# A hybrid RWKV-7 and sliding-window decoder block in exact float32: the early up blocks' second product added at once, and the row-factor passes set in a fixed order

## The chip, the cores and the metric

One core of a Trainium2 chip runs the whole program. The metric is the time of one execution on the device in microseconds (us), as the median of several runs. Instructions are issued in order on each engine: TensorE (PE: matmuls, and PEld: weight loads), VectorE (DVE), ScalarE (ACT), GpSimd (POOL) and SyncE (SP). In this kernel POOL and SP do little more than start transfers.

## The reference

The block takes `x` of 512 rows by 2048 columns. It is normalised and multiplied by `w_in`; RWKV-7 time mixing and sliding-window attention work on the result; gates merge the two, `w_out` brings them back, and the sum with `x` is `x1`. The stage of this change begins there: `x1` is normalised by its root mean square and `norm2_g`, multiplied by `w_up` (2048 by 2 x 5632), passed through a causal convolution of width 3 along the rows, gated, and multiplied by `w_down`.

```python
x = x + (g_rw * p_rw + g_att * p_att) @ w_out[l]
x = x + conv_ffn(rms_norm(x, norm2_g[l]), w_up[l], conv_w[l], conv_b[l], w_down[l])
# conv_ffn(h, ...):
u = h @ w_up
up = jnp.pad(u, ((0, 0), (CONV_W - 1, 0), (0, 0)))
c = up[:, 0:S] * conv_w[0] + up[:, 1:S + 1] * conv_w[1] + up[:, 2:S + 2] * conv_w[2] + conv_b
val, gate = jnp.split(c, 2, axis=-1)
return (jax.nn.silu(gate) * val) @ w_down
```

## The kernel before

**Products.** The three large products after attention (`w_out`, `w_up`, `w_down`) are made by a Strassen-Winograd scheme: both factors are cut in quarters, and seven products of quarters (with sums of quarters as factors) take the place of eight. Float32 accuracy comes from splitting each factor into a high and a low part, so that one product is three matmuls per tile: high by high, high by low, low by high.

**The up stage.** `w_up` is worked in 44 blocks, one per 128 value columns and the 128 gate columns that go with them. A block `f` has the seven products P1, P2, P7, P6, P5, Q4, P3, and one of them is 24 matmuls of 128x128 by 128x256. `parts` (L1087, L1088) splits the weights of a product: ACT writes the rounded high part `whi`, then DVE subtracts for the low part `wlo`. For P6 and P3 DVE first adds two quarters (`sums`, L1081). `hlp` has three buffers for the split weights, so the split of a product waits until the product three before it is through. The weights come by SP in 512 KB quarters (L1072) into a ring of six `raw` buffers and two `a11` buffers; for `s1` and `s3` POOL then starts a second transfer that adds another quarter on arrival (L1074). A load is issued when a buffer becomes free.

**Row factors.** The other factor is the normalised `x1`, in quarters `q11`, `q12`, `q21`, `q22` (in the rows of instructions: `x_13037`, `x_13038`, `x_13039`, `x_13040`). They are transposed on PE, and `transposed` copies the result from PSUM times `norm2_g`, half of the copies on ACT and half on DVE. For `q12` and `q22` the transposing matmul is against a diagonal that holds the rows' scale (`dg`). Sums of quarters are the factors `t3`, `t1`, `t2`, `t4`, each an op on DVE over 128x2048. Every factor is then split by `split_q`: high part on ACT (L1052, 1.9 us), low part on DVE (L1053, 2.3 us). `b11` belongs to P1, `b21` to P2, `t3` to P7, `t2` to P6, `t1` to P5, `t4` to Q4, `b22` to P3.

**Order of products.** The first four blocks are the early ones: P1 for all four, then P2 for all four, then P7, since `b11` and `b21` are there first. Then come the remaining products of blocks 0 and 1 in turns, P6(0), P5(0), P6(1), P3(0), P5(1), Q4(0), P3(1), Q4(1), and the same for blocks 2 and 3. From block 4 on all seven follow each other. In an early block P1 goes to one half of a PSUM bank (`X`) and is copied to `t1`-named tile `t_15888` and so on by ACT (L1114); P2 goes to the other half of the same bank (`Z`), and P6 and P5 later accumulate on `X`. The sum of both, the first part of `u`, is written by DVE from the copy and from `Z` (`B[f].out("P2")`, L1125): for blocks 0 and 1 just ahead of P6(0), for 2 and 3 after P6(2) and Q4(2). While the main loop runs, `prep` for product i+2 (sum and split) is written ahead of the matmuls of product i, and the copies out of PSUM (`out`, L1121 to L1125) behind them.

**What sets the order.** The kernel is built on a scheduler that may reorder instructions inside an engine. `pin` keeps an instruction in the order of the source; the matmuls, weight splits and copies out are pinned, the row-factor ops (`transposed`, `split_q`, the sums of quarters) are not. `reuse_waits` on the pools makes a new tile wait until the last user of the memory is through.

## Time and profile before

| | us |
|---|---|
| median of 3 runs | 2936.24 (2934.93 to 2939.33) |
| the profiled execution's own time | 2935.18 |
| its span, first to last instruction | 2933.4 |
| PE busy | 2879.3 (98%) |
| DVE busy | 1959.2 (67%) |
| ACT busy | 1319.0 (45%) |

The profiled execution is 1.06 us under the median. Times in the rows are counted from the start of the span. PE is busy for 98% of it, so it is the few gaps of PE that can be won or widened, and they differ from stage to stage. The early up blocks lie between 1595 and 1700 us.

### The profile page before, as it was taken

To read this page: it belongs to the slowest core of one execution; us is meant where nothing else is said; L and a number is where in the kernel's file an instruction comes from. 1 tells how busy PE (TensorE), PEld (TensorE's weight loads), DVE (VectorE), ACT (ScalarE), POOL (GpSimd) and SP (SyncE) were. 2 spreads that over 40 slices of the span, in tenths; PEclk is the share of its full clock that TensorE was granted. 3 is DMA by queue.
4 is the path that set the end of the run, shared out by engine and by line. 5 is a ranking of instruction groups with operands and counts; after the bars stand their busy time and mean duration, and the time that the engine had idled before them with its cause. 6 is when DMAs were issued, how large, how long until landed. Compare 5 with 4: busy or idle time off the path is not lost.

```text
span 2933.4 us, 48233 instructions
## 1 busy us (share of the span) xinstructions
PE 2879.3 (98%) x18810; PEld 2453.2 (84%) x18810; DVE 1959.2 (67%) x3250; ACT 1319.0 (45%) x2134; POOL 219.4 (7%) x288
## 2 busy tenths in 40 slices
PE   7999999999999999999999899999999999999999
PEld 6777777777777777788888899999999999888887
DVE  5565666667667666345567877777877877665555
ACT  4344434434434434232356555555555554544444
POOL 0001000000000000101000011101101010000000
PEclk9999999999999999999999999999999999999999
DMA  6865656656656656878877788888889888877785
GB/s 184 212 152 149 175 141 159 162 134 160 163 138 160 158 139 168 274 217 247 286 249 236 195 234 238 237 230 226 226 236 242 233 227 228 313 239 243 255 258 188
DMA packets 225141, 609.39 MB, mean 208 GB/s; under 512 B 24768, under 2 KB 44944, under 8 KB 223888
## 3 DMA queue, kind: packets, MB, share of 16 engines
q1 hardware_dynamic: 157504, 434.86, 46.8%
q0 software_dynamic: 36064, 132.14, 23.5%
q10 hardware_dynamic: 31344, 39.31, 3.9%
q8 instruction: 147, 2.41, 0.3%
q14 instruction: 82, 0.67, 0.1%
HBM read 556.56 MB, written 174.43 MB: 249 GB/s over the span
## 4 chain that ended last, share of the span: by engine, by line
PE 91%; DVE 3%; DMA 3%; ACT 2%; issue 1%; ACTq 0%; SPq 0%; DVEq 0%; POOLq 0%
PE X L1105 16%; PE X L972 11%; PE acc L261 11%; PE acc L260 10%; PE acc L259 10%; PE Y L972 8%; PE Y L1105 8%; PE Z L1105 4%; PE bulk L686 1%; DMA raw<-in_w_up_dram 1%; PE mi L504 1%; PE bulk L748 1%; PE psG L755 1%; PE psS L766 1%; PE bulk L725 1%
## 5 line engine op out<-in xcount | busy, mean ns | idle before, releaser
L259 PE MATMUL acc<-xhi,whi 128*128 128x512 f32 x1120 | 456.1, 407 | 5.2 <-ACT whi L242 5.2
L261 PE MATMUL acc<-xhi,wlo 128*128 128x512 f32 x1120 | 459.4, 410 | 1.7 <-DVE wlo L243 1.7
L260 PE MATMUL acc<-xlo,whi 128*128 128x512 f32 x1120 | 452.7, 404 | 0.0
L242 ACT ACTIVATE whi<-raw 128x512 fp32r<-128x512 f32 x352 | 220.1, 629 | 478.0 <-PE acc L260 368.5
L965 DVE TENSOR_TENSOR wlo<-raw,whi 128x1024 fp32r<-128x1024 f32 x210 | 257.1, 1225 | 203.6 <-ACT whi L964 201.9
L243 DVE TENSOR_TENSOR wlo<-raw,whi 128x512 fp32r<-128x512 f32 x352 | 239.8, 688 | 198.9 <-ACT whi L242 191.2
L964 ACT ACTIVATE whi<-raw 128x1024 fp32r<-128x1024 f32 x210 | 222.6, 1060 | 289.1 <-PE X L972 150.6
L1105 PE MATMUL X<-b,whi 128*128 128x256 f32 x1472 | 269.2, 283 | 2.3 <-DVE u L1125 0.9
L1105 PE MATMUL X<-t,whi 128*128 128x256 f32 x1408 | 259.8, 285 | 10.1 <-DVE u L1125 9.6
L1088 DVE TENSOR_TENSOR wlo<-raw,whi 128x1024 fp32r<-128x1024 f32 x176 | 215.0, 1223 | 77.0 <-ACT whi L1087 76.9
L1105 PE MATMUL Y<-t,whi 128*128 128x256 f32 x1408 | 257.2, 283 | 0.0
L259 PEld LDWEIGHTS acc<-xhi,whi 128*128 128x128 f32 x1120 | 211.3, 189 | 44.8 <-ACT whi L242 6.4
L261 PEld LDWEIGHTS acc<-xhi,wlo 128*128 128x128 f32 x1120 | 211.0, 188 | 44.9 <-DVE wlo L243 4.4
L260 PEld LDWEIGHTS acc<-xlo,whi 128*128 128x128 f32 x1120 | 211.0, 188 | 40.4 <-issue 1.6
L1087 ACT ACTIVATE whi<-a 128x1024 fp32r<-128x1024 f32 x132 | 139.4, 1056 | 216.6 <-DVE a L1081 214.7
L1105 PEld LDWEIGHTS X<-b,whi 128*128 128x128 f32 x1472 | 229.5, 192 | 3.1 <-issue 2.4
L1105 PEld LDWEIGHTS X<-t,whi 128*128 128x128 f32 x1408 | 221.7, 194 | 10.7 <-DVE u L1125 7.1
L1105 PEld LDWEIGHTS Y<-t,whi 128*128 128x128 f32 x1408 | 219.6, 192 | 0.0
L1105 PE MATMUL X<-b,wlo 128*128 128x256 f32 x736 | 208.5, 283 | 2.3 <-DVE wlo L1088 2.3
L1088 DVE TENSOR_TENSOR wlo<-a,whi 128x1024 fp32r<-128x1024 f32 x132 | 161.7, 1225 | 67.4 <-ACT whi L1087 66.7
L1105 PE MATMUL X<-t,wlo 128*128 128x256 f32 x704 | 200.4, 285 | 0.2 <-DVE wlo L1088 0.2
L1105 PE MATMUL Y<-t,wlo 128*128 128x256 f32 x704 | 199.2, 283 | 0.0
(347 smaller groups left out, 6117.7 us busy)
## 6 DMA issues: line engine op xcount, KB each, us to landing
raw<-in_w_up_dram SPq DMA_DIRECT2D x180, 512.0 KB
raw<-in_w_z_dram SPq DMA_DIRECT2D x288, 256.0 KB
s_dn<-in_w_dn_dram POOLq DMA_DIRECT2D x88, 512.0 KB, 6.7
raw<-in_w_up_dram POOLq DMA_DIRECT2D x88, 512.0 KB, 8.6
raw<-s_dn SPq DMA_DIRECT2D x88, 512.0 KB
raw<-in_w_dn_dram SPq DMA_DIRECT2D x66, 512.0 KB
a<-in_w_up_dram SPq DMA_DIRECT2D x48, 512.0 KB
s_dn<-in_w_dn_dram SPq DMA_DIRECT2D x44, 512.0 KB
```

Of the source, the lines that this page charges most:

```text
L242: pin(act.activation(hi, raw, AF.Copy))
L243: pin(dve.tensor_tensor(lo, raw, hi.bitcast(F32), op=ALU.subtract))
L259: pe.matmul(acc, whi[:, j], xhi[:, k], start=first, stop=False)
L260: pe.matmul(acc, whi[:, j], xlo[:, k], start=False, stop=False)
L261: pe.matmul(acc, wlo[:, j], xhi[:, k], start=False, stop=last)
L504: pe.matmul(ps[:, h], pT[:, kb, h], vt[:, n - 1 + kb, g * HD : (g + 1) * HD], start=kb == kbs[0], stop=kb == kbs[-1])
L964: act.activation(whi, wr, AF.Copy)
L965: dve.tensor_tensor(wlo, wr, whi.bitcast(F32), op=ALU.subtract)
L972: pe.matmul(dst, l[:, q, ts], r[:, es], start=fst and j == 0, stop=lst and j == 2, skip_group_check=True)
L1087: pin(act.activation(hi, t, AF.Copy))
L1088: pin(dve.tensor_tensor(lo, t, hi.bitcast(F32), op=ALU.subtract))
L1105: pin(pe.matmul(ps, l[:, k], r[:, k], start=start and k + i == 0, stop=last and i == 2, skip_group_check=True))
```

## The change

1. In `transposed`, DVE takes one copy in four instead of one in two when the diagonal is used (`q12`, `q22`), ACT the others; these copies are pinned.
2. All row-factor ops are pinned. `split_q` falls into `high` (ACT) and `low` (DVE), and they are written in a fixed order around the products: at most one factor's pass per product.
3. In an early block, P2 is added to the ACT copy of P1 as soon as it is there (`self.t1 += Z`, DVE). `begin` later copies that sum into `u` on ACT, without reading PSUM. Four adds and four copies take the place of four adds.
4. The last factor's split (`t4`) is moved behind P6(0) and P5(0); the factor `q21` stays ahead of P6(0) in the source.

```diff
             dst = q[:, 2 * k // KH, k % (KH // 2) * TH : (k % (KH // 2) + 1) * TH]
-            if k % 2:
-                dve.tensor_scalar(dst, src, g, None, op0=ALU.mult)
+            if k % (4 if dg else 2) == 1:
+                pin(dve.tensor_scalar(dst, src, g, None, op0=ALU.mult))
             else:
-                act.activation(dst, src, AF.Copy, scale=g)
+                pin(act.activation(dst, src, AF.Copy, scale=g))
...
+    def high(n, q):
+        pin(act.activation(halves(bq[n][0]), q, AF.Copy))
+
+    def low(n, q):
+        hi, lo = (halves(x) for x in bq[n])
+        pin(dve.tensor_tensor(lo, q, hi.bitcast(F32), op=ALU.subtract))
...
+            if n == "P2" and self.f < NPRE:
+                pin(dve.tensor_tensor(self.t1, self.t1, Z, op=ALU.add))
+                return
...
+        def begin(self):
+            pin(act.activation(us[self.f % 2][:, 0, 2 : 2 + TH], self.t1, AF.Copy))
...
-        if n != "P2" or f >= NPRE:
-            B[f].out(n)
+        B[f].out(n)
...
     run(3)
-    dve.tensor_tensor(q11, q11, q12, op=ALU.subtract)
     transposed(tps, 1, q22, dg)
     tpx.close()
+    pin(dve.tensor_tensor(q11, q11, q12, op=ALU.subtract))
     run(4)
-    dve.tensor_tensor(q12, q22, q12, op=ALU.subtract)
-    split_q("t3", q12)
+    pin(dve.tensor_tensor(q12, q22, q12, op=ALU.subtract))
+    high("t3", q12)
+    run(5)
+    low("t3", q12)
     tcx.close()
     x1q.close()
-    run(5)
+    high("t1", q11)
     run(6)
-    split_q("t1", q11)
+    low("t1", q11)
     run(7)
...
+    pin(dve.scalar_tensor_tensor(q11, q11, -1.0, q22, op0=ALU.mult, op1=ALU.subtract))
+    high("t2", q11)
     run(8)
-    dve.scalar_tensor_tensor(q11, q11, -1.0, q22, op0=ALU.mult, op1=ALU.subtract)
-    split_q("t2", q11)
+    high("b22", q22)
     run(9)
+    low("t2", q11)
     run(10)
-    split_q("b22", q22)
+    low("b22", q22)
     run(11)
-    dve.scalar_tensor_tensor(q21, q11, -1.0, q21, op0=ALU.mult, op1=ALU.subtract)
-    split_q("t4", q21)
-    x1s.close()
+    pin(dve.scalar_tensor_tensor(q21, q11, -1.0, q21, op0=ALU.mult, op1=ALU.subtract))
...
+    for f in range(2):
+        B[f].begin()
+    run(3 * NPRE)
+    high("t4", q21)
+    run(3 * NPRE + 1)
+    low("t4", q21)
...
-            B[2 + (steps[i][1] == "Q4")].out("P2")
+            B[2 + (steps[i][1] == "Q4")].begin()
```

**Place one: DVE from the sum `q22 - q12` to the low part of `t2`, the time of P2(2) to P7(3).** `x01_13038` is `q12`, `x00_13037` is `q11`, `x11_13040` is `q22`; `t31_15848` is the low part of `t3`, `t21_15850` of `t2`, `t11_15846` of `t1`. `wlo` from `raw_15813` belongs to P2(3), from `raw_15815`, `raw_15818`, `raw_15947` and `raw_16009` to P7 of blocks 0 to 3. Before:

```order
L1265 TENSOR_TENSOR x01_13038<-x11_13040,x01_13038 128x2048
L1275 SCALAR_TENSOR_TENSOR x00_13037<-x00_13037,x11_13040 128x2048
L1053 TENSOR_TENSOR t31_15848<-x01_13038,t30_15847 128x2048
L1088 TENSOR_TENSOR wlo_16108<-raw_15813,whi_16107 128x1024
L1088 TENSOR_TENSOR wlo_16138<-raw_15815,whi_16137 128x1024
L1088 TENSOR_TENSOR wlo_16172<-raw_15818,whi_16171 128x1024
L1053 TENSOR_TENSOR t21_15850<-x00_13037,t20_15849 128x2048
L1088 TENSOR_TENSOR wlo_16206<-raw_15947,whi_16205 128x1024
```

and in the changed kernel:

```order
L1276 TENSOR_TENSOR x01_13038<-x11_13040,x01_13038 128x2048
L1094 TENSOR_TENSOR wlo_16106<-raw_15813,whi_16105 128x1024
L1119 TENSOR_TENSOR t1_15941<-t1_15941,X_15916 128x256
L1055 TENSOR_TENSOR t31_15848<-x01_13038,t30_15847 128x2048
L1094 TENSOR_TENSOR wlo_16141<-raw_15815,whi_16140 128x1024
L1119 TENSOR_TENSOR t1_15975<-t1_15975,X_15950 128x256
L1055 TENSOR_TENSOR t11_15846<-x00_13037,t10_15845 128x2048
L1094 TENSOR_TENSOR wlo_16175<-raw_15818,whi_16174 128x1024
L1119 TENSOR_TENSOR t1_16039<-t1_16039,X_16014 128x256
L1287 SCALAR_TENSOR_TENSOR x00_13037<-x00_13037,x11_13040 128x2048
L1094 TENSOR_TENSOR wlo_16212<-raw_15947,whi_16211 128x1024
```

The sum for `t2` (L1275, now L1287) and the low part of `t1` (which stood a few rows ahead of these) have moved between the weight splits, and each sum is now followed directly by a weight split.

On ACT at the same place the high parts stand before the change like this:

```order
L1087 ACTIVATE whi_16071<-raw_15811 128x1024
L1052 ACTIVATE b220_15843<-x11_13040 128x2048
L1052 ACTIVATE t30_15847<-x01_13038 128x2048
L1087 ACTIVATE whi_16107<-raw_15813 128x1024
L1087 ACTIVATE whi_16137<-raw_15815 128x1024
L1087 ACTIVATE whi_16171<-raw_15818 128x1024
L1052 ACTIVATE t20_15849<-x00_13037 128x2048
L1087 ACTIVATE whi_16205<-raw_15947 128x1024
```

and in the changed kernel:

```order
L1093 ACTIVATE whi_16071<-raw_15811 128x1024
L1051 ACTIVATE t30_15847<-x01_13038 128x2048
L1093 ACTIVATE whi_16105<-raw_15813 128x1024
L1051 ACTIVATE t10_15845<-x00_13037 128x2048
L1093 ACTIVATE whi_16140<-raw_15815 128x1024
L1093 ACTIVATE whi_16174<-raw_15818 128x1024
L1051 ACTIVATE t20_15849<-x00_13037 128x2048
L1093 ACTIVATE whi_16211<-raw_15947 128x1024
L1051 ACTIVATE b220_15843<-x11_13040 128x2048
L1093 ACTIVATE whi_16243<-raw_16009 128x1024
```

On both engines a sum's high part (ACT, needs the DVE sum) stands ahead of the weight split that the next DVE row waits for, as it did before the change too; what has moved is the DVE work that stood between the two.

**Place two: DVE around P6(0), P5(0) and P6(1).** `a11_16012` is the sum of block 0 (P6), `a11_16143` and in the changed kernel `a11_16146` that of block 1; `raw_16075` are the weights of P5(0); `x10_13039` is `q21`, `t41_15852` the low part of `t4`, `b221_15844` that of `b22`. Before:

```order
L1053 TENSOR_TENSOR b221_15844<-x11_13040,b220_15843 128x2048
L1088 TENSOR_TENSOR wlo_16240<-raw_16009,whi_16239 128x1024
L1081 TENSOR_TENSOR a11_16012<-a11_16012,raw_16075 128x1024
L1281 SCALAR_TENSOR_TENSOR x10_13039<-x00_13037,x10_13039 128x2048
L1088 TENSOR_TENSOR wlo_16272<-a11_16012,whi_16271 128x1024
L1088 TENSOR_TENSOR wlo_16303<-raw_16075,whi_16302 128x1024
L1053 TENSOR_TENSOR t41_15852<-x10_13039,t40_15851 128x2048
L1125 TENSOR_TENSOR u0_16338<-t1_15888,X_15863 128x256
L1125 TENSOR_TENSOR u1_16340<-t1_15941,X_15916 128x256
L1081 TENSOR_TENSOR a11_16143<-a11_16143,raw_16175 128x1024
```

and in the changed kernel:

```order
L1094 TENSOR_TENSOR wlo_16244<-raw_16009,whi_16243 128x1024
L1055 TENSOR_TENSOR t21_15850<-x00_13037,t20_15849 128x2048
L1087 TENSOR_TENSOR a11_16012<-a11_16012,raw_16075 128x1024
L1094 TENSOR_TENSOR wlo_16277<-a11_16012,whi_16276 128x1024
L1055 TENSOR_TENSOR b221_15844<-x11_13040,b220_15843 128x2048
L1094 TENSOR_TENSOR wlo_16307<-raw_16075,whi_16306 128x1024
L1296 SCALAR_TENSOR_TENSOR x10_13039<-x00_13037,x10_13039 128x2048
L1087 TENSOR_TENSOR a11_16146<-a11_16146,raw_16178 128x1024
L1094 TENSOR_TENSOR wlo_16347<-a11_16146,whi_16346 128x1024
```

The low part of `b22` and the sum for `t4` have moved behind the split for P6(0), and stand ahead of the sum for P6(1).

On ACT in the changed kernel the copy of P6(0) out of PSUM (L1130, from `X_15863`) stands behind the high part for P6(1) (`whi_16346`), and the two `begin` copies (L1137) ahead of it:

```order
L1093 ACTIVATE whi_16306<-raw_16075 128x1024
L1137 ACTIVATE u0_16339<-t1_15888 128x256
L1137 ACTIVATE u1_16341<-t1_15941 128x256
L1093 ACTIVATE whi_16346<-a11_16146 128x1024
L1130 ACTIVATE u0_16339<-X_15863 128x256
L1051 ACTIVATE t40_15851<-x10_13039 128x2048
```

Before, the copy of P6(0) stood in the same way behind the high part for P6(1):

```order
L1087 ACTIVATE whi_16302<-raw_16075 128x1024
L1052 ACTIVATE t40_15851<-x10_13039 128x2048
L1087 ACTIVATE whi_16351<-a11_16143 128x1024
L1121 ACTIVATE u0_16338<-X_15863 128x256
L1087 ACTIVATE whi_16381<-a11_16012 128x1024
```

So the place of the copy out is the same in both; what has changed is how much DVE work stands ahead of the sum that the high part needs.

More of the change, by code (lines that the diff above doesn't have):

```diff
@@ L1041, in transposed @@
             dst = q[:, 2 * k // KH, k % (KH // 2) * TH : (k % (KH // 2) + 1) * TH]
-            if k % 2:
-                dve.tensor_scalar(dst, src, g, None, op0=ALU.mult)
+            if k % (4 if dg else 2) == 1:
+                pin(dve.tensor_scalar(dst, src, g, None, op0=ALU.mult))
             else:
-                act.activation(dst, src, AF.Copy, scale=g)
+                pin(act.activation(dst, src, AF.Copy, scale=g))
     def halves(t):
         return t.rearrange("p (a k) s -> p a (k s)", a=2)
+    def high(n, q):
[3 more added lines that the diff above has]
+        pin(dve.tensor_tensor(lo, q, hi.bitcast(F32), op=ALU.subtract))
     def split_q(n, q):
-        hi, lo = (halves(x) for x in bq[n])
-        act.activation(hi, q, AF.Copy)
-        dve.tensor_tensor(lo, q, hi.bitcast(F32), op=ALU.subtract)
+        high(n, q)
+        low(n, q)
     us = []
@@ L1124, in out @@
             else:
-                pin(dve.tensor_tensor(u, self.t1 if n == "P2" and self.f < NPRE else u, ps, op=ALU.add))
+                pin(dve.tensor_tensor(u, u, ps, op=ALU.add))
+        def begin(self):
+            pin(act.activation(us[self.f % 2][:, 0, 2 : 2 + TH], self.t1, AF.Copy))
         def conv(self, part):
@@ L1288, in block_kernel @@
         us.append(u)
+    for f in range(2):
[4 more added lines that the diff above has]
+    low("t4", q21)
+    x1s.close()
     upcx = ExitStack()
@@ L1291, in block_kernel @@
     hp0 = upcx.enter_context(tc.tile_pool(name="hhl0", bufs=1, side="right", reuse_waits="tile"))
-    for f in range(2):
-        B[f].out("P2")
-    for i in range(3 * NPRE, len(steps)):
+    for i in range(3 * NPRE + 2, len(steps)):
         run(i)
         if steps[i] in ((2, "P6"), (2, "Q4")):
-            B[2 + (steps[i][1] == "Q4")].out("P2")
+            B[2 + (steps[i][1] == "Q4")].begin()
         if steps[i] == (NF - 2, "P7"):
```

## The prediction

> **What bounds the kernel now.** I read the page first, then the waits of PE by stage, the busy time by stage, and last the queues row by row where PE waits.
>
> ```profile
> PE 2879.3 (98%) x18810; PEld 2453.2 (84%) x18810; DVE 1959.2 (67%) x3250; ACT 1319.0 (45%) x2134; POOL 219.4 (7%) x288
> PE X L1105 <- DVE u L1125: 10.6, 3, 6.9
> PE X L1105 <- DVE wlo L1088: 2.1, 1, 2.1
> PE X L972 <- ACT u L1121: 1.0, 1, 1.0
> PE X L1105 <- DVE wlo L1088: 0.4, 2, 0.2
> ```
>
> PE is the bound. The second and third row are waits of PE in the early up blocks (1585 to 1720 us), the last two are all that it waits from 1720 to the end. So what the change does happens before 1720, and behind it PE carries the offset to the end, since no slack is left there that could swallow it.
>
> ```profile
> 1620.00:1640.00 20.00, 17.39 (x143) 16.98 (x142) 20.00 (x14) 12.35 (x10) 1.85 (x4) 1.00 0.89 224
> 1640.31:1643.09 2.78, 0.00 (x1) 0.03 (x1) 2.78 (x4) 0.00 (x0) 0.00 (x0) 1.00 0.60 175
> 1669.96:1672.30 2.34, 0.00 (x0) 0.00 (x0) 1.09 (x3) 0.00 (x0) 0.00 (x0) 1.00 0.69 159
> 1672.40:1676.82 4.42, 0.01 (x1) 0.01 (x1) 3.81 (x6) 2.03 (x3) 0.86 (x1) 0.50 0.28 59
> 1676.82:1682.50 5.68, 5.68 (x26) 5.68 (x27) 3.62 (x4) 2.44 (x4) 0.50 (x1) 0.50 0.73 177
> ```
>
> Behind the length of a stretch stand the busy times of PE, PEld, DVE, ACT and POOL, then the granted clock. From 1620 to 1640 DVE is busy for 20.00 of 20.00 us: there DVE sets the pace, and it holds it because none of its rows waits. The other rows are two gaps of PE. In the gap of 2.78 us the clock stays at 1.00. In the one of 6.86 us it falls to 0.50 after 2.4 us and stays there 5.68 us into the next products, which costs half of that, 2.8 us.
>
> ```profile
> 1625.91 0.39 PE L1105 MATMUL X<-b,wlo 128*128 128x256 f32 x1 [2.14 <-DVE wlo L1088]
> 1643.09 0.36 PE L1105 MATMUL X<-t,whi 128*128 128x256 f32 x1 [2.78 <-DVE u L1125]
> 1646.67 0.38 PE L1105 MATMUL X<-t,whi 128*128 128x256 f32 x1 [0.47 <-ACT u L1121]
> 1676.82 0.79 PE L1105 MATMUL X<-t,whi 128*128 128x256 f32 x2 [6.86 <-DVE u L1125]
> 1694.92 0.47 PE L1105 MATMUL X<-b,whi 128*128 128x256 f32 x2 [0.94 <-DVE u L1125]
> 1703.80 2.88 PE Y L1105 x24
> ```
>
> These are PE's gaps (in brackets) by product: 1625.91 is P2(3), 1643.09 P6(0), 1646.67 P5(0), 1676.82 P5(2), 1694.92 P3(3). The last row, of the chain that ended last, is one product: 2.88 us.
>
> **The price of single steps.** DVE's and ACT's rows of before give the durations:
>
> ```profile
> 1608.84 2.29 DVE L1261 TENSOR_TENSOR x<-x,x 128x2048 f32<-128x2048 f32 x1
> 1615.33 1.65 DVE L1043 TENSOR_SCALAR x<-ps_t,par 128x256 f32<-128x256 f32 x4
> 1618.03 2.29 DVE L1265 TENSOR_TENSOR x<-x,x 128x2048 f32<-128x2048 f32 x1
> 1620.23 2.29 DVE L1275 SCALAR_TENSOR_TENSOR x<-x,x 128x2048 f32<-128x2048 f32 x1
> 1624.64 3.49 DVE L1088 TENSOR_TENSOR wlo<-raw,whi 128x1024 fp32r<-128x1024 f32 x3
> 1630.24 1.22 DVE L1088 TENSOR_TENSOR wlo<-raw,whi 128x1024 fp32r<-128x1024 f32 x1
> 1642.53 0.74 DVE L1125 TENSOR_TENSOR u<-t,X 128x256 f32<-128x256 f32 x2
> 1643.19 1.22 DVE L1081 TENSOR_TENSOR a<-a,raw 128x1024 f32<-128x1024 f32 x1
> 1654.08 1.23 DVE L1088 TENSOR_TENSOR wlo<-raw,whi 128x1024 fp32r<-128x1024 f32 x1 [1.65 <-ACT whi L1087]
> 1605.09 0.47 ACT L1045 ACTIVATE x<-ps_t,par 128x256 f32<-128x256 f32 x1 [0.51 <-PE ps_t L1036]
> 1620.35 1.92 ACT L1052 ACTIVATE t<-x 128x2048 fp32r<-128x2048 f32 x1 [1.41 <-DVE x L1265]
> 1622.17 2.93 ACT L1087 ACTIVATE whi<-raw 128x1024 fp32r<-128x1024 f32 x3
> 1646.23 0.38 ACT L1121 ACTIVATE u<-X 128x256 f32<-128x256 f32 x1 [0.65 <-PE X L1105]
> ```
>
> A pass of DVE over 128x2048 is 2.29 us, over 128x1024 1.22 us (three in a row 3.49, so the next starts 1.14 behind), a PSUM copy 0.41, an add of the kind of L1125 0.37. ACT's high part of a factor is 1.92, of a product's weights 1.05 (three 2.93), a copy out 0.38.
>
> **The change part by part.** By count DVE gains: four PSUM copies go to ACT (4 x 0.41 = 1.6 us less), the low part of `t4` (2.3 us) goes behind P6(0), and four adds come where two stood (0.7 us more): 3.2 us less ahead of P6(1)'s sum. ACT gains four copies of 0.47 and four of 0.38, and is 12.35 of 20 us busy, so its own time isn't the question. What counts is the order. In front of every weight split DVE now meets a sum whose high part ACT must make before the split's own high part: DVE hands to ACT, waits for two ACT rows, and has nothing between them. Before, other passes lay there. I walked both queues in the changed order with the durations above (the same walk with the order of before gives 1643.1, 1646.6 and 1676.7 for P6(0), P5(0), P5(2), against the rows' 1643.09, 1646.67, 1676.82). Times at the end of a step, estimates for the changed kernel:
>
> ```
> step (engine)                        before   after   what it waits for
> second copies of q22 (DVE)          1616.98  1615.3   ACT's copies ahead of it
> q11-q12 (DVE)                       1611.13  1617.5   stands behind those copies now
> q22-q12 (DVE)                       1620.3   1621.2   P2(2) split and one add ahead
> high t3, high P2(3) (ACT)                    1624.1   DVE idle 3.0
> split P2(3) (DVE)                   1625.9   1625.4
> low t3, P7(0), low t1, P7(1), 2 adds         1633.0   no idle
> sum for t2 (DVE)                    1622.5   1635.3
> high t2, high P7(2) (ACT)                    1638.2   DVE idle 3.0
> split P7(2) (DVE)                   1631.46  1639.4
> high b22, high P7(3) (ACT)                   1640.9   DVE idle 1.6
> split P7(3), low t2, sum P6(0) (DVE)         1645.5
> high, low P6(0)                              1647.9   DVE idle 1.3
> start of P6(0) (PE)                 1643.09  1647.8   +4.7
> low b22, split P5(0), q21, sum P6(1) 1644.41 1654.6   no idle
> high P6(1), then copy of P6(0) (ACT)         1656.1
> start of P5(0) (PE)                 1646.67  1656.2   +9.5
> split Q4(0) (DVE)                   1655.31  1665.4   +10.1
> ```
>
> P5(0) accumulates on the PSUM half that ACT must first copy out, and this copy is queued behind the high part for P6(1), whose sum stands on DVE behind `b22`'s low part and `q21`. Ahead of the copy both orders have this high part; before, its sum was done at 1644.41. From P5(0) on, eight products follow without a gap: P6(2) ends at about 1679.2.
>
> Then comes the long gap:
>
> ```profile
> 1655.33 4.46 DMA raw<-in_w_up_dram
> 1660.34 11.74 DMA raw<-in_w_up_dram
> 1672.11 1.24 DVE a L1081
> 1673.45 1.07 ACT whi L1087
> 1674.54 1.22 DVE wlo L1088
> 1676.82 14.29 PE X L1105 x96
> 1675.12 0.36 ACT L1121 ACTIVATE u<-X 128x256 f32<-128x256 f32 x1
> 1655.33 1.46 SPq L1072 DMA_DIRECT2D raw<-in_w_up_dram  x2
> 1658.26 0.84 POOL L227 DMA_DIRECT2D s_dn<-in_w_dn_dram  x1 [12.94 <-DMA s_dn<-s_dn]
> raw<-in_w_up_dram POOLq DMA_DIRECT2D x88, 512.0 KB, 8.6
> ```
>
> The first six are of the chain that ended last. The weights `s1` of block 3 are issued at 1655.33, as soon as the split of Q4(0) frees a buffer (1654.08 + 1.23), land after 4.46 us, and the added quarter after 11.74 more (the page's median is 8.6), behind the transfer of 1658.26 on POOL's queue. Their sum (1672.11) is what ACT's high part for P6(3) waits for, and ACT's copy of P6(2) (1675.12) is queued behind that. So the new `begin` doesn't free P5(2) at 1669.96: the copy of P6(2) holds it until 1675.5, and only the wait from there to 1676.82 goes.
>
> The sum, against the profiled execution's 2935.18 us:
> - the split of Q4(0), and with it `s1` of block 3, later: +10.1.
> - half clock after the worked gap of 5.4 us before P5(0) (1650.7 to 1656.2): bounds 0 (the gap of 2.78 us) and 2.8 (that of 6.86); by length between them 1.9, of which 0.9 is hidden by DVE's own lateness in front of the split: +1.0 (0 to 1.9).
> - POOL's two transfers: the buffer is freed 1.1 us behind P5(1)'s now (two splits in a row) instead of 2.9, so the transfer ahead starts relatively later: bounds 0 and 1.8, middle: +1.0.
> - P5(2) released by ACT's copy and not by DVE's add: -1.3.
> - P3(3) no longer waits for the add of block 3: -0.9 (bounds -0.94 and 0, the split of P3(3) is late next).
> - half clock after P5(2), whose gap is now about 5.5 us: 1.9 instead of 2.8: -0.9 (-2.8 to 0).
>
> Together +9.0, so 2944.2 for such an execution; it stands 1.06 below the median of 2936.24, which gives 2945.2.
>
> Costed at nothing: the four `begin` copies (1.5 us on ACT, the first two while ACT waits for P6(1)'s sum); `t4`'s split (done by about 1663, used by Q4(0) after 1667); the POOL memset of `u`, which waits for `t3`'s low part (1628) and stands ahead of the added quarter for P5(1) that isn't due before 1637; the loads `s1` of blocks 0 and 1, landing 7 us or more ahead of their sums (4.46 and 8.6 us behind the split of P7(1) at 1632.7, for a sum at 1653.4); SP's one exchange of rows (the third quarter of block 3 behind `a11`), 20 us ahead of its use.
>
> **A rule of the Trainium skill on the clock.** The row 1669.96:1672.30 shows full clock for 2.3 us of the gap, the next one half. The Trainium skill, "TensorE: Matmul & The Clock Gate", section "What's actually happening", puts the fall after at least one idle window of about 3.4 us, on a window that runs freely. The trace has the fall sooner, 2.4 us after PE stopped. By the page a gap of 5.5 us holds a whole window about six times in ten (estimate from its figure: 5.5 less 3.4, over 3.4), so its sum would be 2944.2 or 2945.2; the trace makes the fall likely each time.
>
> **Rivals.**
> *Faster: P5(2) is freed at once.* If `begin` takes away the whole wait, P5(2) starts at 1669.96, P6(3) follows when its split is done (1674.54 + 1.22 = 1675.8), and three products later, at 1684.4, the four are through that end at 1691.11 now (1676.82 + 14.29): -6.7, with -0.9 at P3(3) 2928.6. It decides if P6(2) ends no later than today and the copy of P6(2) doesn't stand behind the high part of P6(3). For it: the releaser is named DVE L1125. Against it: ACT's row 1675.12, and the idle time of DVE in the walk. 5 in 100.
> *No change: the long gap swallows the lateness.* If `s1` of block 3 landed at 1672.1 as now, P5(2) would follow P6(2) at about 1681.1 (with the slow stretch), +4.3, without a slow stretch behind it (-2.8) and with -0.9: +0.6, 2936.8. It decides if the buffer comes free independently of DVE's splits; the SP row at 1655.33 says it doesn't. 11 in 100.
> *Slower still.* The gaps before P7(2) (2.7 us and more) and P6(0) also halve the clock, and the two slow stretches in the sum reach 2.8: up to +15, 2947 to 2952. 10 in 100.
> *My forecast*, +3.3 to +13.8 (the bounds above, 1.5 us of error in the walk, and the spread of the runs): 2939.5 to 2950. 74 in 100.
>
> **How the numbers follow.** 0.2% is 5.9 us, about what a measurement of this kernel can tell from no change. Slower by more: the forecast but for its low end (70) and slower still (10), 80. Within: no change (11) and that low end (4), 15. Faster: 5. The range reaches from 2938.5 to 2952, which leaves out the faster case and most of no change.
>
> **What would show it.** Right: DVE waits for ACT's `whi` in pieces of some 3 us before P2(3) and P7(2); P6(0) starts near 1648; P5(0) has a gap of about 5 us, released by ACT's copy; the gap before P5(2) remains, released by ACT and no longer by DVE, with half clock behind it; from 1720 on the rows are those of before, some 9 us later. Wrong: DVE busy throughout from 1620 to 1650, P5(0) before 1650, or `s1` of block 3 landing near 1672.

## The result, and the profile after

| | before | changed |
|---|---|---|
| median, us | 2936.74 (2932.53 to 2939.33, 8 runs) | 2943.75 (2941.15 to 2946.57, 8 runs) |
| ratio | | 1.0024, 95% interval 1.0014 to 1.0034: 4.1 to 10.0 us slower |
| profiled execution, us | 2935.18 | 2946.57 |

The change costs 7 us by the medians. A second comparison gave 2943.65 against 2933.68, ratio 1.0034 (1.0022 to 1.0047), which is 10 us.

First the line of busy times from the page of the changed kernel, then the waits of its PE, three of those from 1585 to 1720 us and the two from 1720 to the end:

```profile
PE 2887.6 (98%) x18810; PEld 2460.4 (84%) x18810; DVE 1957.5 (66%) x3246; ACT 1321.1 (45%) x2142; POOL 219.8 (7%) x288
```

```profile
PE X L1111 <- ACT u L1130: 11.8, 2, 6.6
PE Y L1111 <- ACT whi L1093: 2.5, 1, 2.5
PE X L1111 <- ACT whi L1093: 1.4, 1, 1.4
...
PE X L972 <- ACT u L1130: 1.2, 1, 1.2
PE X L1111 <- DVE wlo L1094: 0.2, 1, 0.2
```

Where DVE's add (L1125) held PE for 10.6 us in three pieces, ACT's copy out (now L1130) holds it for 11.8 in two. Of the two waits for ACT's high parts (now L1093; the low parts are L1094) the one of 2.5 us, before P7(2), is new, and the one of 1.4, before P2(3), was 0.5. From 1720 on PE waits for 1.4 us in both kernels. The start of the first up product, P1(0), differs from one execution to the next (1591.5 to 1597.2 us in the profiles below; the source ahead of it is the same, and two profiles of the changed kernel alone have 1595.6 and 1591.5). From P2(4), which is the fourth product of block 4 to run, to the end all profiles have 1222.6 to 1225.0 us. So from here on times are counted from P1(0). The busy times of that stretch, P1(0) to P2(4), of before and of the changed kernel:

```profile
1595.29:1709.39 114.10, 100.44 (x808) 99.28 (x809) 90.48 (x108) 59.46 (x80) 11.32 (x15) 0.96 0.81 220
```

```profile
1595.55:1720.85 125.30, 106.48 (x808) 104.17 (x809) 89.18 (x104) 61.43 (x88) 11.17 (x15) 0.92 0.74 199
1641.00:1647.80 6.80, 6.80 (x42) 6.80 (x42) 5.38 (x4) 2.09 (x3) 0.00 (x0) 0.68 0.57 177
1656.38:1664.60 8.22, 8.22 (x46) 8.22 (x47) 5.57 (x5) 4.14 (x4) 0.21 (x1) 0.63 0.76 191
1688.97:1696.60 7.63, 7.63 (x48) 7.63 (x49) 5.99 (x9) 3.88 (x6) 0.86 (x1) 0.72 0.72 158
```

The stretch is 11.2 us longer in this pair: PE idles 5.2 us more (125.30 - 106.48 = 18.82 against 13.66), and its busy time is 6.0 longer for the same 808 matmuls, because three stretches at half clock (lower three rows) stand where one stood. DVE has less to do (89.18 us, was 90.48) and idles 12.5 us more (36.1 against 23.6). On what, the groups of DVE say, first of before, then changed; behind the second bar is the idle time ahead of the group and what ended it:

```profile
L1088 DVE TENSOR_TENSOR wlo<-raw,whi 128x1024 fp32r<-128x1024 f32 x18 | 21.8, 1221 | 3.6 <-ACT whi L1087 3.6
L1088 DVE TENSOR_TENSOR wlo<-a,whi 128x1024 fp32r<-128x1024 f32 x14 | 17.0, 1223 | 8.4 <-ACT whi L1087 8.4
```

```profile
L1094 DVE TENSOR_TENSOR wlo<-raw,whi 128x1024 fp32r<-128x1024 f32 x18 | 22.0, 1222 | 10.0 <-ACT whi L1093 9.9
L1094 DVE TENSOR_TENSOR wlo<-a,whi 128x1024 fp32r<-128x1024 f32 x14 | 17.1, 1224 | 12.2 <-ACT whi L1093 12.2
```

In front of the same 32 splits DVE waits 22.1 us for ACT's high part instead of 12.0. PE's gaps by product, P7(2), P6(0) (no gap), P5(0), P5(2), P6(4), and the rows of DVE and ACT behind them:

```profile
1638.49 0.73 PE L1111 MATMUL Y<-t,whi 128*128 128x256 f32 x2 [2.52 <-ACT whi L1093]
1647.85 0.40 PE L1111 MATMUL X<-t,whi 128*128 128x256 f32 x2
1656.38 0.80 PE L1111 MATMUL X<-t,whi 128*128 128x256 f32 x2 [5.22 <-ACT u L1130]
1688.97 0.80 PE L1111 MATMUL X<-t,whi 128*128 128x256 f32 x2 [6.63 <-ACT u L1130]
1718.11 0.39 PE L1111 MATMUL X<-t,wlo 128*128 128x256 f32 x1 [0.49 <-DVE wlo L1094]
```

```profile
1624.45 1.23 DVE L1094 TENSOR_TENSOR wlo<-raw,whi 128x1024 fp32r<-128x1024 f32 x1 [2.99 <-ACT whi L1093]
1638.47 1.22 DVE L1094 TENSOR_TENSOR wlo<-raw,whi 128x1024 fp32r<-128x1024 f32 x1 [2.92 <-ACT whi L1093]
1655.00 1.06 ACT L1093 ACTIVATE whi<-a 128x1024 fp32r<-128x1024 f32 x1 [6.49 <-DVE a L1087]
1655.96 0.37 ACT L1130 ACTIVATE u<-X 128x256 f32<-128x256 f32 x1
1662.33 0.42 DVE L1132 TENSOR_TENSOR u<-u,Y 128x256 f32<-128x256 f32 x1 [1.47 <-ACT u L1130]
1666.47 1.22 DVE L1094 TENSOR_TENSOR wlo<-raw,whi 128x1024 fp32r<-128x1024 f32 x1 [0.39 <-ACT whi L1093]
1685.55 1.23 DVE L1087 TENSOR_TENSOR a<-a,raw 128x1024 f32<-128x1024 f32 x1 [2.32 <-DMA raw<-in_w_up_dram]
```

And the transfer ahead of that last row, from the chain that ended last:

```profile
1673.67 11.86 DMA raw<-in_w_up_dram
```

The waits before P2(3) and P7(2) are there (2.99, 2.92), ACT's copy stands behind the high part for P6(1), the split of Q4(0) (1666.47) ends at 1667.69, and the quarter added to `s1` of block 3 comes at 1685.55.

### The profile page after: what moved, and what is told of

Its sections match the earlier page's. It is cut to its first block, busy times and chain, and to the rows that moved or that the text cites. A ratio compares the mean times of both kernels' runs of the same rounds, so it can differ in the third digit from the quotient of the medians.

```text
span 2944.8 us, 48232 instructions
## 1 busy us (share of the span) xinstructions
PE 2887.6 (98%) x18810; PEld 2460.4 (84%) x18810; DVE 1957.5 (66%) x3246; ACT 1321.1 (45%) x2142; POOL 219.8 (7%) x288
## 4 chain that ended last, share of the span: by engine, by line
PE 85%; issue 6%; DVE 4%; ACT 2%; DMA 2%; POOL 0%; SPq 0%; ACTq 0%; POOLq 0%; DVEq 0%
PE X L1111 16%; PE acc L261 10%; PE acc L260 10%; PE acc L259 10%; PE X L972 8%; PE Y L1111 8%; PE Y L972 6%; PE Z L1111 4%; PE bulk L686 1%; PE mi L504 1%; PE bulk L748 1%; PE psG L755 1%; PE psS L766 1%; DMA raw<-in_w_z_dram 1%; PE bulk L725 1%
## 5 line engine op out<-in xcount | busy, mean ns | idle before, releaser
L1111 PE MATMUL X<-t,whi 128*128 128x256 f32 x1408 | 261.9, 286 | 12.0 <-ACT u L1130 11.8
L1094 DVE TENSOR_TENSOR wlo<-raw,whi 128x1024 fp32r<-128x1024 f32 x176 | 215.1, 1222 | 83.1 <-ACT whi L1093 83.0
L1093 ACT ACTIVATE whi<-a 128x1024 fp32r<-128x1024 f32 x132 | 139.4, 1056 | 223.4 <-DVE a L1087 218.5
L1094 DVE TENSOR_TENSOR wlo<-a,whi 128x1024 fp32r<-128x1024 f32 x132 | 161.7, 1225 | 71.3 <-ACT whi L1093 70.6
```

Source lines behind the costliest of these rows:

```text
L1093: pin(act.activation(hi, t, AF.Copy))
L1094: pin(dve.tensor_tensor(lo, t, hi.bitcast(F32), op=ALU.subtract))
L1111: pin(pe.matmul(ps, l[:, k], r[:, k], start=start and k + i == 0, stop=last and i == 2, skip_group_check=True))
```

## The experiments

Each kernel was timed 5 to 11 times, but for the second profile of before, which is a single execution. "Us to before" is the difference of the medians in the same comparison (comparisons were made on several chips, so kernels are set against each other by this column), with the interval of the ratio; the sections are from the profile of each: P1(0) to P5(0), P5(0) to P5(2), P5(2) to P2(4), and their sum.

| kernel | us to before | interval of the ratio | to P5(0) | to P5(2) | to P2(4) | sum |
|---|---|---|---|---|---|---|
| before | | | 51.38 | 30.15 | 32.57 | 114.10 |
| before, second profile | | | 54.24 | 28.96 | 31.50 | 114.70 |
| changed | +7.0 | 1.0014 to 1.0034 | 60.83 | 32.59 | 31.88 | 125.30 |
| changed, again | +10.0 | 1.0022 to 1.0047 | 60.85 | 31.40 | 31.94 | 124.19 |
| 1 part 3 alone | +2.3 | 0.9998 to 1.0016 | 55.38 | 28.79 | 32.13 | 116.30 |
| 2 without part 3 | +11.2 | 1.0026 to 1.0051 | 62.34 | 30.88 | 32.16 | 125.38 |
| 3 `q21` later | +8.1 | 1.0016 to 1.0040 | 58.63 | 32.16 | 31.82 | 122.61 |
| 4 high parts behind | +5.2 | 1.0005 to 1.0023 | 55.69 | 30.43 | 32.00 | 118.12 |
| 5 copies first | +10.1 | 1.0025 to 1.0050 | 56.09 | 27.88 | 38.06 | 122.03 |
| 6 POOL's transfer later | +7.9 | 1.0018 to 1.0041 | 60.84 | 29.70 | 32.66 | 123.20 |
| 7 part 3, copies first | +0.3 | 0.9995 to 1.0013 | 51.40 | 26.37 | 37.62 | 115.39 |
| 8 sums early | -3.7 | 0.9979 to 0.9996 | 46.97 | 26.11 | 37.42 | 110.50 |
| 9 gaps filled | +9.8 | 1.0020 to 1.0045 | 61.14 | 29.33 | 31.84 | 122.31 |
| 10 sums early, POOL's transfer later | -5.2 | 0.9971 to 0.9989 | 46.97 | 26.85 | 35.44 | 109.26 |

**1. Part 3 alone.** To the kernel before:

```diff
+            if n == "P2" and self.f < NPRE:
+                pin(dve.tensor_tensor(self.t1, self.t1, Z, op=ALU.add))
+                return
...
-            B[f].out("P2")
+            B[f].begin()
```

> The kernel before with part 3 of the change alone: the second product is added at once (four adds on VectorE where two stood before P7) and copied into u later by ScalarE; the row-factor passes stay as before. Theory (the lateness comes from the order of the row-factor passes): little is lost, P6(0) starts near 1642 and P5(0) near 1647 to 1650 (before 1643.1 and 1646.7; changed 1647.9 and 1656.4), the time is 0 to 2 us over before. Rival (the four early adds, and P5(0) being released by a ScalarE copy that queues behind a high part, are the cost): P5(0) after 1654 and 6 us or more over before.

```profile
1649.53 0.80 PE L1105 MATMUL X<-t,whi 128*128 128x256 f32 x2 [5.63 <-ACT u L1124]
1678.32 0.79 PE L1105 MATMUL X<-t,whi 128*128 128x256 f32 x2 [4.23 <-ACT u L1124]
```

P6(0) starts at 46.7 (before: 47.8) and P5(0) at 55.38, which is 1650.7 on the first profile's clock, a little over the bound. Both gaps are now released by ACT's copy out. The time is 2.3 us over before, with an interval that includes no change. So part 3 is not what costs 7 to 10 us. The scheduler placed the unpinned passes anew in this build (the sum for `t4` now stands right ahead of its own low part, where DVE waits 1.98 us for ACT's high part), so these 2.3 us are not the add's own price.

**2. Without part 3.** The changed kernel with the adds where they were before:

```diff
-            if n == "P2" and self.f < NPRE:
-                pin(dve.tensor_tensor(self.t1, self.t1, Z, op=ALU.add))
-                return
...
-        B[f].begin()
+        B[f].out("P2")
```

> The changed kernel without part 3: the second product is added ahead of P6(0) (blocks 0 and 1) and after P6(2) and Q4(2) as in the kernel before; the fixed order of the row-factor passes, the later t4 and the copies moved to ScalarE stay. Theory (the order is the cost): P6(0) at 1648 or later, P5(0) 1656 to 1658, the long gap before P5(2) released again by VectorE's add, the time as in the changed kernel or up to 3 us over it, 7 to 10 us over before. Rival (part 3 is the cost): P5(0) before 1650 and the time within 3 us of before.

```profile
1651.60 0.77 PE L1111 MATMUL X<-t,whi 128*128 128x256 f32 x2 [7.23 <-DVE u L1131]
```

P5(0) comes at 62.3 and the time is 11.2 us over before: parts 1, 2 and 4 without part 3 cost as much as the whole change. This run doesn't separate them, but version 8 below keeps part 1 and is faster than before, so what is left is the order of the passes (parts 2 and 4). Without the early adds P6(0) waits 7.23 us for DVE and P5(0) comes 1.5 us later, but the stretch (125.38) is as long as in the changed kernel; whether the adds help in this order stays open.

**3. The sum `q21` later.**

```diff
     run(11)
-    pin(dve.scalar_tensor_tensor(q21, q11, -1.0, q21, op0=ALU.mult, op1=ALU.subtract))
...
     run(3 * NPRE)
+    pin(dve.scalar_tensor_tensor(q21, q11, -1.0, q21, op0=ALU.mult, op1=ALU.subtract))
     high("t4", q21)
```

> The changed kernel with one pass moved: the sum into q21 (2.3 us on VectorE) stands behind P5(0)'s weight split and P6(1)'s sum instead of ahead of that sum. My prediction named this pass as one of two ahead of P6(1)'s sum, whose high part is ahead of the copy that frees P5(0). Theory: P5(0) comes 2.3 us sooner, at 1654.0, and P5(1) and the rest of VectorE's queue get the 2.3 us back as they still must do that pass before the split of Q4(0): the time falls by 0 to 1 us. Rival (what ScalarE does before P5(0) sets the whole lateness): the split of Q4(0) 2 us sooner too, and the time 2 to 4 us under the changed kernel.

```profile
1653.29 0.50 PE L1111 MATMUL X<-t,whi 128*128 128x256 f32 x2 [3.02 <-ACT u L1130]
1663.03 2.35 DVE L1094 TENSOR_TENSOR wlo<-raw,whi 128x1024 fp32r<-128x1024 f32 x2
```

P5(0) comes 2.2 us sooner, as expected. The split of Q4(0) ends at 70.7 (1665.38), 1.0 to 1.4 us sooner than in the changed kernel, between the two theories. The time, +8.1 to before, lies between the changed kernel's two, +7.0 and +10.0: these runs can't tell.

**4. High parts behind.** Four rows of ACT (the high parts of `t3`, `t1`, `t2` and `b22`) move behind the next product's `whi`; `run` calls its second argument between the split and the matmuls:

```diff
-    high("t3", q12)
-    run(5)
+    run(5, lambda: high("t3", q12))
...
-    high("t2", q11)
-    run(8)
-    high("b22", q22)
-    run(9)
+    run(8, lambda: high("t2", q11))
+    run(9, lambda: high("b22", q22))
```

> The changed kernel with four rows of ScalarE moved and nothing on VectorE: the high parts of t3, t1, t2 and b22 stand behind the high part of the next product's weights instead of ahead of it. Theory (VectorE hands a sum to ScalarE and waits for two ScalarE rows, the factor's of 1.9 us and the weights' of 1.1 us): VectorE's waits of about 3 us before the splits of P2(3) and P7(2) vanish or shrink under 1 us, P6(0) starts near 1643, P5(0) near 1651, and the time falls 5 us, to 1 to 3 us over before. Rival (VectorE has simply too much to do ahead of P6(0), or the weights land late): P6(0) still at 1646 or later and the time within 2 us of the changed kernel.

```profile
1619.70 1.22 DVE L1094 TENSOR_TENSOR wlo<-raw,whi 128x1024 fp32r<-128x1024 f32 x1
1621.83 2.29 DVE L1055 TENSOR_TENSOR t<-x,t 128x2048 fp32r<-128x2048 f32 x1 [0.58 <-ACT t L1051]
1631.37 1.22 DVE L1094 TENSOR_TENSOR wlo<-raw,whi 128x1024 fp32r<-128x1024 f32 x1
1634.38 1.23 DVE L1094 TENSOR_TENSOR wlo<-raw,whi 128x1024 fp32r<-128x1024 f32 x1 [1.79 <-ACT whi L1093]
1649.54 0.80 PE L1111 MATMUL X<-t,whi 128*128 128x256 f32 x2 [5.22 <-ACT u L1130]
```

The splits of P2(3) (1619.70) and P7(2) (1631.37) no longer wait at all; they waited 2.99 and 2.92 us. What is left is 0.58 ahead of `t3`'s low part and 1.79 ahead of the split of P7(3), which waited 1.52 in the changed kernel. P6(0) starts at 46.3 instead of 51.5 to 52.3, P5(0) at 55.7 instead of 60.8, and the stretch is 6 to 7 us shorter. The medians show less, +5.2 to before instead of +7.0 and +10.0, and not the 1 to 3 that I had expected. Not one instruction of DVE was moved or saved for that. So the mechanism up to P6(0) is the order in which DVE and ACT hand over to each other, not the load of either. The gap of 5.22 before P5(0) is the same in both kernels: it isn't made by these four rows.

**5. Copies first.** The copies out of P6(0) and P6(2) are queued ahead of the next product's split:

```diff
     def run(i, copy_first=False):
         f, n = steps[i]
+        if copy_first:
+            B[f].mm(n)
+            B[f].out(n)
         prep(i + 2, 2 if 3 * NPRE <= i < 7 * NPRE else 1)
...
-    run(3 * NPRE)
+    run(3 * NPRE, copy_first=True)
...
-        run(i)
+        run(i, copy_first=steps[i] == (2, "P6"))
```

> The changed kernel with the copies out of P6(0) and P6(2) (ScalarE, 0.38 us each) queued ahead of the next product's split instead of behind it; no other row moves. It tests whether the copy that frees P5(0) and P5(2) is held by its place in ScalarE's queue. Theory: P6(0) stays at 1647.8, P5(0) starts 3.5 us behind it at 1651.4 with no gap (changed: 1656.4 after 5.2 us), P5(2) near 1679 instead of 1689; but P6(1) and P6(3) then wait for their own splits, which are as late as in the changed kernel, so the time falls by only 3 us (the half-clock stretches and the order of the waits), to about 4 us over before. Rival (the place of the copy is the whole lateness): P6(1) follows P5(0) without a gap and the time is within 1 us of before.

```profile
1649.55 0.50 PE L1111 MATMUL X<-t,whi 128*128 128x256 f32 x2 [0.47 <-ACT u L1130]
1654.01 0.50 PE L1111 MATMUL X<-t,whi 128*128 128x256 f32 x2 [1.33 <-ACT whi L1093]
1682.71 0.50 PE L1111 MATMUL X<-t,whi 128*128 128x256 f32 x2 [2.15 <-ACT whi L1093]
```

P5(0) starts 4.7 us sooner, with no gap but the copy's own 0.47; then P6(1) (1654.01) and P6(3) (1682.71) wait for their splits. Sections two and three together grow by 1.5 to 2.6 us, and the stretch is 2.2 to 3.3 us shorter. The times don't show that: +10.1 to before, in runs spread over 7 us.

**6. POOL's transfer later.** The first pair of transfers for the down projection goes out later: SP's copy after P5(2) instead of after P3(0), POOL's added quarter after P3(2) instead of after P3(1):

```diff
+        if (f, n) == (2, "P5"):
+            wp["first"] = sums_along()
+        if (f, n) == (2, "P3"):
+            wp["first"]()
-        if n == "P3":
+        if n == "P3" and f > 1:
```

> The changed kernel with the first transfer of down-projection weights (the pair of SyncE's copy and GpSimd's added quarter at 1671 in the changed trace, ahead of the added quarter for s1 of block 3) moved some 20 us later. My sum has +1.0 us for the two transfers of GpSimd. Theory: the added quarter lands 3 us sooner after its issue (about 8.6 instead of 11.9 us), VectorE's wait of 2.3 us for it ahead of P6(3)'s sum vanishes, the gap before P5(2) shrinks from 6.6 to about 4.3 us and the time falls by 2 to 3 us. Rival (another engine's queue is late next, or the transfer is no faster alone): the gap stays over 6 us and the time within 1 us of the changed kernel.

```profile
1671.91 0.86 POOL L1080 DMA_DIRECT2D raw<-in_w_up_dram  x1 [15.51 <-DMA raw<-in_w_up_dram]
...
1682.51 1.22 DVE L1087 TENSOR_TENSOR a<-a,raw 128x1024 f32<-128x1024 f32 x1
1685.93 0.80 PE L1111 MATMUL X<-t,whi 128*128 128x256 f32 x2 [4.23 <-ACT u L1130]
```

DVE's wait of 2.32 us for the quarter is gone, and the gap before P5(2) is 4.23 us (was 6.63 and, in the second profile, 5.89). The stretch is only 1.0 to 2.1 us shorter, since section three takes 0.8 more. In the trace that is the expected mechanism, somewhat under the expected size; the time, +7.9 to before, can't be told from the changed kernel's.

**7. Part 3 in the old order, copies first.** Edits 1 and 5 together, on the kernel before.

> The order of the row-factor passes as in the kernel before, the second product added at once (part 3 alone), and the copies out of P6(0) and P6(2) ahead of the next split. With the first of these runs (part 3 alone: P5(0) at 1649.5 after a gap of 5.6 us, P5(2) at 1678.3 after 4.2 us, both released by that copy) it shows what part 3 is worth when nothing stands ahead of the copy. Theory: P5(0) starts at 1645 to 1647, P5(2) at 1671 to 1673, smaller gaps before P6(1) and P6(3) take part of it back; the time is 2 to 4 us under before. Rival (P6(1) and P6(3) wait for the same splits as long, so that only the place of the gap changes): within 1 us of before.

```profile
1647.87 0.50 PE L1105 MATMUL X<-t,whi 128*128 128x256 f32 x2 [0.60 <-ACT whi L1087]
1675.33 0.50 PE L1105 MATMUL X<-t,whi 128*128 128x256 f32 x2 [1.70 <-ACT whi L1087]
```

My theory fell. Against run 1 P5(0) comes 4.0 us sooner and P5(2) 6.4 sooner, P2(4) only 0.9: P6(1) and P6(3) (the rows) and the products behind them wait instead, as the rival has it. Freeing P5's half bank sooner gains next to nothing while DVE's queue stays.

**8. Sums early.** The passes in another fixed order, the high parts behind as in edit 4 and the copies first as in edit 5; `later` holds passes that `prep` writes between a product's sum and its split:

```diff
     transposed(tps, 0, q12, dg)
+    pin(dve.tensor_tensor(q11, q11, q12, op=ALU.subtract))
     run(3)
+    high("t1", q11)
+    low("t1", q11)
     transposed(tps, 1, q22, dg)
     tpx.close()
...
     pin(dve.tensor_tensor(q12, q22, q12, op=ALU.subtract))
+    pin(dve.scalar_tensor_tensor(q11, q11, -1.0, q22, op0=ALU.mult, op1=ALU.subtract))
+    run(5, lambda: (high("t3", q12), high("t2", q11)))
...
+    later.append(lambda: low("b22", q22))
...
+    later.append(lambda: pin(dve.scalar_tensor_tensor(q21, q11, -1.0, q21, op0=ALU.mult, op1=ALU.subtract)))
+    run(3 * NPRE, lambda: high("t4", q21), True)
+    later.append(lambda: low("t4", q21))
```

> The changed kernel with its passes in another fixed order: the sums for t1, t3 and t2 earlier (t1 between the transposes of the two quarters, t2's sum right behind t3's), the high parts of the factors behind the next split's on ScalarE, the low parts of b22 and t4 and the sum q21 each between a product's sum and its split, so that VectorE has work while ScalarE makes the high part, and the copies out of P6(0) and P6(2) ahead of the next split. No pass is left out. Theory (the loss is only the order in which VectorE and ScalarE hand over to each other): P6(0) near 1639, P5(0) near 1642, P5(2) near 1668, and the time 6 to 9 us under before. Rival (VectorE's load ahead of P6(0) or the landing of weights sets these times whatever the order): P6(0) after 1642 and the time within 2 us of before.

```profile
1670.31 0.50 PE L1111 MATMUL X<-t,whi 128*128 128x256 f32 x2 [0.53 <-ACT u L1130]
1672.56 1.23 DVE L1087 TENSOR_TENSOR a<-a,raw 128x1024 f32<-128x1024 f32 x1 [1.89 <-DMA raw<-in_w_up_dram]
1674.93 0.51 PE L1111 MATMUL X<-t,whi 128*128 128x256 f32 x2 [1.50 <-ACT whi L1093]
```

On the first profile's clock P6(0) is at 1638.8, P5(0) at 1642.3, P5(2) at 1668.4: all three as expected. The time is 3.7 us under before (1.2 to 6.2), less than expected: behind P5(2) DVE waits 1.89 us for the quarter added to `s1` of block 3, P6(3) waits with it, and a stretch at half clock follows.

**The changed kernel again, and 9: gaps filled.** Matmuls that nobody reads stand in the two long gaps:

```diff
+            if (self.f, n) in ((0, "P6"), (2, "P6")):
+                for k in range(36 if self.f == 0 else 44):
+                    pin(pe.matmul(B[self.f + 1].Z, whi[:, k % KH], xh[:, k % KH], start=False, stop=False, skip_group_check=True))
```

> The changed kernel as it is, on the chip of the runs beside it, for a second profile and a common measure. Theory: the order of events before P1 of block 4 is fixed by VectorE's and ScalarE's queues, so P6(0), P5(0) and the gaps are as in the first profile within 0.3 us, counted from the first up product; what differs from execution to execution are the half-clock stretches (three in the first profile, 2.9, 2.9 and 2.1 us lost), so the time lies 7 to 11 us over before. Rival (the lateness itself varies): P5(0) or P5(2) more than 1 us elsewhere.

> The changed kernel with extra matmuls that nobody reads in its two long gaps: 36 behind P6(0) (4.3 us at full clock) and 44 behind P6(2) (5.3 us), into the half bank of the next block's second product, which has been taken out by then. They wait for nothing and end ahead of the copy that frees P5. It takes away the half clock behind the gaps and nothing else. Theory (my sum has half clock behind both gaps as a cost): P5(0) starts when it did, is through in 2.9 instead of 4.3 us with P6(1) behind it, the clock stays at 1.00 from 1656 on, s1 of block 3 is issued 2 us sooner, P5(2) starts 2 us sooner, and the time falls by 4 to 6 us against the changed kernel. Rival (the half clock is hidden by VectorE's own lateness): within 1.5 us of the changed kernel.

The second profile of the changed kernel, then two windows of the run with the gaps filled, P5(0) to P5(2) and P5(2) to P2(4), and that run's splits of P5(1) and Q4(0):

```profile
1652.38 0.80 PE L1111 MATMUL X<-t,whi 128*128 128x256 f32 x2 [5.23 <-ACT u L1130]
1683.78 0.80 PE L1111 MATMUL X<-t,whi 128*128 128x256 f32 x2 [5.89 <-ACT u L1130]
```

```profile
1656.95:1686.28 29.33, 28.48 (x238) 28.27 (x236) 21.61 (x23) 15.75 (x21) 2.60 (x3) 1.00 0.81 216
1686.28:1718.12 31.84, 29.93 (x241) 29.12 (x242) 25.17 (x33) 15.43 (x24) 3.45 (x4) 1.00 0.93 257
```

```profile
1663.61 2.35 DVE L1094 TENSOR_TENSOR wlo<-raw,whi 128x1024 fp32r<-128x1024 f32 x2
```

P5(0) repeats within 0.02 us (60.83, 60.85), P5(2) differs by 1.2 and P6(0) by 0.8. With the gaps filled the clock is 1.00 in both sections. P5(0) itself comes 0.3 later. Section two then takes 29.33 us instead of 31.40 and 32.59, 2.1 to 3.3 us less. Of that the half clock behind P5(0) is 1.6 to 2.0: so much sooner, counted from P1(0), the split of Q4(0) ends (70.15, with 71.71 and 72.14 in the two profiles of the changed kernel). The rest is P5(0)'s later start and the time from that split to the sum for P6(3), 16.90 us instead of 17.11 and 17.86. Section three takes 31.84 instead of 31.88 and 31.94: the half clock behind P5(2) costs next to nothing. DVE and ACT set the pace there, and PE waits in small pieces once it is faster: from the sum for P6(3) to one and the same weight split near the end of the section DVE takes 31.24 us with the gap filled (1682.86 to 1714.10) and 31.29 without (1685.55 to 1716.84). The stretch is 1.9 to 3.0 us shorter; I had expected 4 to 6, and the medians (2943.44 and 2943.65) are the same within their spread. So the traces show the 2 to 3 us, the times don't.

**The kernel before again.**

> The kernel before as it is, for a second profile. Theory (VectorE's and ScalarE's queues fix the order of events, the half-clock stretches vary from one execution to the next): counted from the first up product, P6(0), P5(0) and the start of the long gap lie as in the first profile unless a gap halves the clock that did not there (the one of 2.8 us before P6(0) is the candidate, and costs up to 2.9 us), so the stretch from the first up product to the second product of block 4 takes 114 to 118 us (first profile 114.1), and the comparison of the two first profiles, 11.2 us, is at the upper end of what the change costs. Rival (the half clock falls at the same places each time): 114.1 within 0.3 us, and the clock at full speed before 1672.

Windows of the wait before P2(3) and of the 2.5 us that start 1 us behind it, first in the first profile, then in the second:

```profile
1623.27:1625.91 2.64, 0.50 (x3) 0.29 (x3) 2.64 (x3) 2.64 (x3) 0.65 (x3) 1.00 1.00 152
...
1626.90:1629.40 2.50, 2.50 (x23) 2.50 (x23) 2.50 (x3) 0.70 (x2) 0.00 (x0) 1.00 1.03 308
```

```profile
1622.85:1625.49 2.64, 0.50 (x3) 0.30 (x3) 2.64 (x3) 2.64 (x3) 0.73 (x3) 1.00 0.93 126
...
1626.50:1629.00 2.50, 2.50 (x15) 2.50 (x14) 2.50 (x3) 0.00 (x0) 0.00 (x0) 0.56 1.00 318
```

The same kernel, the same gap, full clock in one execution and half in the other. The second execution has half clock behind P2(3)'s gap, P6(0)'s and P5(2)'s, the first only behind P5(2)'s. P6(0) comes 1.5 us later for it and P5(0) 2.9, and at P2(4) 0.6 is left. Before and changed thus differ by 9.5 to 11.2 us over their four profiles, which agrees with the second comparison of medians (+10.0) and touches the interval of the first.

**10. Sums early, and POOL's transfer later.** Edits 8 and 6 together.

> The order with the sums early and the copies first (the version that was 3.7 us under before) with the first transfer of down-projection weights moved some 20 us later on SyncE and GpSimd. In that version's trace VectorE waits 1.9 us at 1672.6 for the added quarter of s1 of block 3, GpSimd issues it behind that transfer, and the clock then falls for 3.3 us. Theory: that wait and the gap of 1.5 us before P6(3) vanish, the half-clock stretch too, and the time is 5 to 8 us under before. Rival (VectorE's and ScalarE's queue is late there anyway): P6(3)'s gap stays over 1 us and the time is 3 to 4 us under before.

```profile
1670.65 1.22 DVE L1087 TENSOR_TENSOR a<-a,raw 128x1024 f32<-128x1024 f32 x1
1679.31 0.80 PE L1111 MATMUL X<-b,whi 128*128 128x256 f32 x2 [2.15 <-ACT u L1130]
```

DVE no longer waits for the quarter, P6(3)'s gap before its high part is gone, section three is 2.0 us shorter, and the time is 5.2 us under before (3.2 to 8.5). Half clock is still there, behind P3(2)'s gap of 2.15 us. This version beats both kernels, 15 us under the changed one in the same comparison.

## Why the prediction was right, and where its terms were off

I had predicted 2945.2, slower, and the reason: in front of the splits DVE hands a sum to ACT and waits for two of its rows. The run with those ACT rows moved, and nothing else, shows it: both waits are gone, and 5.1 of the 9.5 us before P5(0) with them. Step by step:

- **P6(0) +4.7, P5(0) +9.5.** Measured +4.5 and +9.45 (second profile +3.7 and +9.47). The +4.5 is partly luck: P6(0) starts on the high part and needn't wait for the whole split, at 51.5 in the second profile and with the gaps filled; in the first profile PE itself was later, at half clock behind P7(2). The waits that the walk put before P2(3) and P7(2) (3.0 each) are 2.99 and 2.92; the releaser of P5(0) is the copy behind P6(1)'s high part, as written.
- **Split of Q4(0) +10.1.** Measured +12.1 (72.14 against 60.02 from P1(0); second profile +11.7). The walk kept the clock full, and at full clock it is right: with the gap before P5(0) filled the split ends at 70.15 (1663.61 + 2.35, less 1595.81), +10.1. What comes on top is the next term.
- **Half clock behind P5(0) +1.0 (0 to 1.9).** This is the term that was mis-sized: 2.0 us, 1.6 in the second profile, at the upper end of the bounds. It holds the copy of P5(0), and DVE stands 1.47 us for that copy (row 1662.33) ahead of the split. The price by the gap's length, 1.9, was too low: P5(0) and P6(1) take 8.53 and 8.07 us together in the two profiles, where two products at full clock take 5.76, so 2.8 and 2.3 us are lost. Of these 0.8 and 0.7 are hidden, about the 0.9 that I had set.
- **POOL's two transfers +1.0.** From the end of the split of Q4(0) to the sum 17.86 us (1667.69 to 1685.55) against 16.80: +1.1. The second profiles have 17.11 and, before, 15.61, so the term lies between +0.3 and +2.3. The run with the transfer moved gives 1.0 to 2.1 back.
- **P5(2) freed by ACT's copy -1.3.** From the sum for P6(3) to P5(2) there are 3.42 us (1685.55 to 1688.97) against 4.71 (1672.11 to 1676.82): -1.3. The releaser is ACT's copy, the gap remains. P5(2) came +11.9 and +10.7, predicted +10.8.
- **P3(3) no longer waits -0.9, half clock behind P5(2) -0.9.** Measured together -0.7. P3(3)'s wait of 0.94 is gone, but P6(4) now waits for its split (row 1718.11), and the half clock there is hidden by DVE: 31.84 us without it, 31.88 with it. Both steps assumed that PE is the bound behind P5(2); for these 32 us DVE and ACT are.
- **Behind P2(4)** nothing was given back, as said.

In the first pair of profiles section two has +2.4 where my terms make +1.3, and section three -0.7 where they make -1.8: so 11.2 instead of 9.0. The other pairs have 9.5 to 10.6. The first comparison's 7.0 is lower than all of them; why, stays open. So the mechanism was right and the sum a little small; that the median, 2943.75, lies within 1.5 us of the forecast is partly luck. Single executions differ by over 5 us in the start of P1(0) alone, which is no part of the change.

**The rivals.** The long gap didn't swallow the lateness: `s1` of block 3 is issued when the split of Q4(0) frees its buffer, in every kernel here. P5(2) wasn't freed at once. "Slower still" had a part of its condition met, half clock behind P7(2)'s gap of 2.52 us in both profiles (P6(0) had no gap), but not its price: P5(0) is at 60.8 all the same, since DVE and not PE sets it, and at 61.1 in the run with the gaps filled, where the clock stays full behind P7(2).

**The rule on the clock.** The Trainium skill, "TensorE: Matmul & The Clock Gate", section "What's actually happening", has the clock fall after at least one idle window of about 3.4 us, on windows that run freely. The second half agrees: in the kernel before the same gap halved the clock in one execution and not in the other. The first doesn't: there PE was busy for 0.50 of 2.64 us, and its longest idle piece was 2.14 us.

## What to carry to other kernels

Where two in-order engines make one result in two steps, write the second engine's instructions in the order in which the first will need them, and give the first something to do between handing over and taking back: four rows of ACT in the wrong order cost 6 to 7 of some 10 us in these traces (2 to 5 by the medians), with no work added. A pass that "fits in the slack" by its engine's busy share can still be on the path; add up who waits for whom, row by row. And freeing a buffer sooner moves a wait unless the queue that is late next is shortened too, so cost the next releaser before claiming the gap.
